# A two-block transformer on one core: the modulation's sums over partitions by 32x32 turns on VectorE and stacked identities, its gates by way of DRAM

## The chip, the core and the metric

The kernel runs on one core of one Trainium2 chip. The metric is the device time of one execution in microseconds (us); a kernel's time is the median of its runs. TensorE (PE) multiplies, VectorE (DVE) and ScalarE (ACT) do the elementwise work, GpSimd (POOL) a few small things, and SyncE (SP) issues nearly all transfers. PEld stands for TensorE's weight loads.

## What is computed

Two transformer blocks over 256 tokens of width 1024, in float32. The second block has two layers. In each, a vector `c` (one for the whole batch) is turned into six vectors of 1024, by which the layer's activations are shifted, scaled and gated. This modulation is what the change is about:

```python
c_act = jax.nn.silu(c)
for i in range(DEPTH_2):                                   # two layers
    mod = (c_act @ ada_w[i] + ada_b[i])[:, None, :]        # 1024 x 6144
    sh_a, sc_a, g_a, sh_f, sc_f, g_f = jnp.split(mod, 6, axis=-1)
    h = rms_norm(x, norm_g[i, 0]) * (1.0 + sc_a) + sh_a
    y = ...                                                # one of two attentions of h
    x = x + g_a * rms_norm(y, norm_g[i, 1])
    h = rms_norm(x, norm_g[i, 2]) * (1.0 + sc_f) + sh_f
    x = x + g_f * rms_norm(swiglu_2(h, ffn_w_in[i], ffn_w_out[i]), norm_g[i, 3])
```

## The kernel before

**The products.** All weights (42 million numbers, and 13 million of the modulation) are read once. SP loads them in tiles `raw` (three buffers, each of four units of 128x512); ACT rounds each unit to a high part `hi`, DVE subtracts to a low part `lo`, and TensorE forms each product from matmuls of high by high, high by low and low by high parts, mostly of 512 columns, through `mm` (line 145 in the profile). Turns of activations are `transpose` calls through `tr` (line 151). `hi` and `lo` have 16 pairs of buffers (`slots`), and further ones (`wp`) in the feed-forward parts.

**What sets the order.** The class `Order` writes the program in one pass. It keeps a clock `o.now` that runs with TensorE's matmuls, and small generators (tasks) are resumed when the clock has reached the time that they gave. `pin` ties each instruction to the one before it on its engine, so the order in which tasks happen to issue is each engine's order on the chip. All work of DVE, ACT and POOL is recorded at line 89, all transfers at line 137. The planned durations only set the order; on the chip every instruction still waits for its own inputs. A transfer carries one of eight completion semaphores in turn, so a transfer also waits until the one eight before it has landed.

**The modulation (`ada`).** The product `c_act @ ada_w` isn't made on TensorE. For each of 12 vectors, in two halves of 512, four transfers bring 128x2x512 weights to `araw`, and DVE adds them into `sums` (tiles `asum`) with 8 `scalar_tensor_tensor` operations by `c_act`. Each of the 128 partitions then holds a part of the sum, and `ada_finish` adds over the partitions, once for each of the 24 halves:

- for the 16 halves of shifts and scales: four 128x128 turns of `sums` on TensorE into a bank, one `reduce_sum` on DVE from the bank to four columns of `fm`, and for the scales one small operation with the norm's gain;
- for the 8 halves of gates: `split` of `sums` to a high and a low part (one ACT copy, one DVE subtraction), two matmuls of 512 columns with an all-ones matrix `ones_r`, which leave the sum in every partition, and one DVE product into a tile `gain` that holds the norm's gain, read by `load_gain` as one row sent to all partitions.

`chain` uses `gain` after a projection or feed-forward part, and `evacuate` uses `fm`.

**The start.** SP issues the halves of `x`, the first four weight units, then seven small transfers of vectors (`rows`, 8 or 12 rows of 128 numbers each, later turned into columns by `turn_rows`), and then the next weight tile.

**An address pad.** `small("pad_end", [P, PAD_END])` takes 104 numbers per partition, so that the tiles allocated behind it (`qp`, `gp`, `wp`) begin at a chosen address.

Of the kernel before, what the change touches and what calls it, by code (L numbers as in the profile page):

```python
# [12 lines left out]
F32 = mybir.dt.float32  # L13
F32R = mybir.dt.float32r
AF = mybir.ActivationFunctionType
OP = mybir.AluOpType
AX = mybir.AxisListType
# [3 lines left out]
P = 128  # L21
D = 1024
# [11 lines left out]
STOCK = 9  # L34
ADA_START, ADA_EARLY, ADA_LATE = 30.0, 5.5, 8.0
HEADS_1, HEADS_2 = 9.0, 2.0
PAD_END = 104
FIRST_DMA, SLOW_BYTES = 1.9, 2.2e6
RATE, SLOW_RATE = 360e3, 270e3
WARM = 6  # L40
# [178 lines left out]
def block_kernel(ctx: ExitStack, tc: tile.TileContext, a: dict, onehot: bass.AP, out: bass.AP):  # L219
    nc = tc.nc  # L220
    o = Order(tc)
    A, V, G = o.A, o.V, o.G
# [4 lines left out]
    dram = ctx.enter_context(tc.tile_pool(name="dram", bufs=1, space=DRAM))  # L227

    def ring(pool, name, n, shape, dtype=F32):
        return Ring([pool.tile(shape, dtype, name=f"{name}{i}") for i in range(n)])  # L230

    def small(name, shape, dtype=F32):
        return cst.tile(shape, dtype, name=name)

    banks = ring(psum, "bank", 8, [P, 512])
    raws = ring(cst, "raw", 3, [P, 2048])
    araws = ring(cst, "araw", 2, [P, 1024])
    slots = Ring([(small(f"hi{i}", [P, 512], F32R), small(f"lo{i}", [P, 512], F32R)) for i in range(16)])
    st = ring(cst, "st", 4, [P, 528])
    ch = ring(cst, "ch", 3, [P, 512])  # L240
    ep = ring(cst, "ep", 4, [P, 384])
    gains = ring(cst, "gain", 2, [P, D])
    asum = ring(cst, "asum", 2, [P, 512])
# [119 lines left out]
    def split(hi, lo, src, after=0.0):  # L363
        t = A.activation(hi, src, AF.Copy, after=after)
        return V.tensor_sub(lo, src, hi.bitcast(F32), after=t)
# [75 lines left out]
    vec = {}  # L441
# [29 lines left out]
    def stay_warm():  # L471

        b = banks.take()
        for _ in range(WARM):
# [8 lines left out]
    later = rows(("c", a["c_2"].rearrange("l (k p) -> (l k) p", p=P), 8),  # L483
                 ("conv", a["conv_w"].rearrange("l t (k p) -> (l t k) p", p=P), 12),
                 ("ffn_pre", a["norm_ffn_pre"].rearrange("l (k p) -> (l k) p", p=P), 8),
                 *((("g", l, i), a["norm_g_2"][l, i].rearrange("(k p) -> k p", p=P), 8) for l in range(2) for i in (0, 2)))
    ident = small("ident", [P, P])
    make_identity(nc, ident)
    tri = small("tri", [P, P])
    nc.vector.memset(tri, 1.0)  # L490
    ones_r = small("ones_r", [P, P], F32R)
# [114 lines left out]
    def load_gain(src, gain):  # L606
        gain.tile = yield from o.get(gains)
        gain.load.t = o.dma(gain.tile, src.to_broadcast([P, D]))


    fm = [small(f"fm{l}", [P, 4, 8]) for l in range(2)]
# [3 lines left out]
    ada_done = {one: [Mark(), Mark()] for one in ada_order}  # L615
    gated = {one: Gain() for one in ada_order if one[1][0] == "g"}
# [2 lines left out]
    c_mark = Mark()  # L619
    c_act = small("c_act", [P, 8])  # L620

    def ada_finish(l, what, cc, sums, r):
        yield r
        c = slice(cc * 512, (cc + 1) * 512)
        if what[0] == "g":
            yield from o.until(gated[l, what].load)
            pair = yield from o.get(slots)
            hv, lv = pair
            r = split(hv, lv, sums)
            asum.give(sums, r)  # L630
            yield r
            tp = yield from o.get(banks)
            o.mm(tp, ones_r, hv, True, False)
            r = o.mm(tp, ones_r, lv, False, True)
            slots.give(pair, r)
            yield r
            dst = gated[l, what].tile[:, c]
            r = V.tensor_mul(dst, dst, tp)
        else:
            tp = yield from o.get(banks)  # L640
            for j in range(4):
                r = o.tr(tp[:, j * P:(j + 1) * P], sums[:, j * P:(j + 1) * P], ident)
            asum.give(sums, r)
            yield r
            i = {"sh_a": 0, "sc_a": 1, "sh_f": 2, "sc_f": 3}[what]
            dst = fm[l][:, i, cc * 4:cc * 4 + 4]
            r = V.reduce_sum(dst, tp.rearrange("p (k c) -> p k c", c=P), axis=AX.X)
            if what[1] == "c":
                yield r
                g = vec["g", l, 0 if what == "sc_a" else 2][:, cc * 4:cc * 4 + 4]  # L650
                r = V.scalar_tensor_tensor(dst, dst, 1.0, g, op0=OP.add, op1=OP.mult)
        banks.give(tp, r)
        ada_done[l, what][cc].t = r

    def ada():
        yield from o.until(c_mark)
        pieces = [(l, what, cc, k0) for l, what in ada_order for cc in range(2) for k0 in range(0, 8, 2)]
        loaded, t0 = [], o.now
        for i in range(len(pieces) + 1):
            if i < len(pieces):  # L660
                l, what, cc, k0 = pieces[i]
                c0 = parts_of.index(what) * D + cc * 512
                if k0 == 0:
                    if what[0] == "g" and cc == 0:
                        o.spawn(load_gain(a["norm_g_2"][l, 1 if what == "g_a" else 3].unsqueeze(0), gated[l, what]))
                    sums = yield from o.get(asum)
                    r = G.memset(sums, 0.0)
                    yield r
                    ba = o.dma(sums[0:1, :], a["ada_b_2"][l:l + 1, c0:c0 + 512])
                t = yield from o.get(araws)  # L670
                arrival = o.dma(t.rearrange("p (k c) -> p k c", c=512),
                                a["ada_w_2"][l].rearrange("(k p) c -> p k c", p=P)[:, k0:k0 + 2, c0:c0 + 512])
                loaded.append((l, what, cc, k0, t, max(arrival, ba), sums))
            if i:
                l, what, cc, k0, t, arrival, s = loaded.pop(0)
                yield max(arrival, t0 + i * ADA_EARLY)
                while (o.urgent or V.free > o.now + SLACK or
                       pos["lo"] - pos["first"] < STOCK and o.now < t0 + i * ADA_LATE):
                    yield o.now + 0.2
                for k in range(2):  # L680
                    r = V.scalar_tensor_tensor(s, t[:, k * 512:(k + 1) * 512], c_act[:, k0 + k:k0 + k + 1], s,
                                               op0=OP.mult, op1=OP.add)
                    yield r - 0.3
                araws.give(t, r)
                if k0 == 6:
                    o.spawn(ada_finish(l, what, cc, s, r), r)


    def scope(**kinds):

        stack, got = ExitStack(), {}
        for name, (n, shape, dtype) in kinds.items():
            got[name] = ring(stack.enter_context(tc.tile_pool(name=name, bufs=1, reuse_waits="tile")), name, n, shape, dtype)
        return stack, got
# [87 lines left out]
    cum, cum_mark = [small(f"cum{h}", [P, 8]) for h in range(2)], [Mark(), Mark()]  # L782
    rows_mark = Mark()

    small("pad_end", [P, PAD_END])
    phase, sc = scope(qp=(4, [P, 4, 256], F32), gp=(8, [P, 512], F32),
                                   mk=(1, [P, 256], F32))
    qks, gp = sc["qp"], sc["gp"]
# [209 lines left out]
    group(take(2), 260, keep_gb, None)  # L998
    o.spawn(gates_of_c())
    o.spawn(ada(), ADA_START)  # L1000
    group(take(2), 512, keep_gc, None)
    group(take(2), 512, make_z, None)
# [428 lines left out]
```

## Time and profile before

| what | us |
|---|---|
| median of 3 runs | 981.91 (981.43 to 982.16) |
| the profiled execution | 983.57 |
| its span, first to last instruction | 981.8 |
| TensorE busy in the span | 970.9 (99%) |
| VectorE busy | 773.7 (79%) |
| ScalarE busy | 622.3 (63%) |

TensorE runs at its full clock throughout (granted clock 0.999). A matmul's row in the profile gives its whole passage through the array, which overlaps the next one's; what it costs the stream is the distance from its start to the next start. Rows of a timeline merge equal instructions that follow each other; an instruction of float32 operands that isn't a turn stands there as two records.

### The profile page before, as it was taken

The numbers are of one execution on the slowest core, as the hardware profiler recorded it, in microseconds if no ns is written. First come the engines' busy times: TensorE is split into PE (matmuls) and PEld (weight loads), VectorE is DVE, ScalarE is ACT, GpSimd is POOL, SyncE is SP. The second block draws the span as 40 slices with busy tenths as digits, with TensorE's granted clock in tenths as the row PEclk, the third lists the DMA queues.
The fourth block names the chain that finished last, engine by engine and source line by source line (L and its number), as shares of the span: only waits on it lengthen the run. The fifth ranks groups of instructions, "written<-read, shape, count | busy, mean of one in ns | idle before, by whom it ended". The sixth has DMA issues, their size and how long they took to land.

```text
span 981.8 us, 14543 instructions
## 1 busy us (share of the span) xinstructions
PE 970.9 (99%) x4986; PEld 810.4 (83%) x4986; DVE 773.7 (79%) x1582; ACT 622.3 (63%) x1390; POOL 34.7 (4%) x65
## 2 busy tenths in 40 slices
PE   8999999999999999999999999999999999999997
PEld 6888778888888888888888888888887888888886
DVE  6689888889999977787899999867686797575742
ACT  6746676775555547866785555557888786565631
POOL 1000000000000001000000000001000100000000
PEclk9999999999999999999999999999999999999999
DMA  7977777669988975766769998874542667646401
GB/s 228 331 258 255 265 273 248 218 229 327 334 294 294 311 263 176 268 223 200 250 205 313 315 318 278 286 258 162 196 142 81 196 198 260 204 162 211 158 28 44
DMA packets 143639, 227.24 MB, mean 231 GB/s; under 512 B 6087, under 2 KB 79028, under 8 KB 143564
## 3 DMA queue, kind: packets, MB, share of 16 engines
q1 hardware_dynamic: 143548, 226.30, 68.6%
q8 instruction: 39, 0.64, 0.3%
q14 instruction: 36, 0.29, 0.1%
q10 hardware_dynamic: 16, 0.00, 0.0%
HBM read 225.22 MB, written 2.63 MB: 232 GB/s over the span
## 4 chain that ended last, share of the span: by engine, by line
PE 93%; issue 2%; DMA 2%; ACT 1%; DVE 1%; SPq 0%; POOL 0%; DVEq 0%; POOLq 0%; ACTq 0%
PE bank L145 89%; PE bank L151 4%; ACT hi L89 1%; DMA bf<-in_b_f_dram 1%; DMA x<-in_x_dram 1%; DVE lo L89 0%; SPq L137 0%; ACT junk L89 0%; DMA raw<-in_w_in_dram 0%; DVE x L89 0%; DVE ch L89 0%; POOL tiny L89 0%; ACT L89 0%; ACT hTb L89 0%; DVE hTb L89 0%
## 5 line engine op out<-in xcount | busy, mean ns | idle before, releaser
L89 DVE TENSOR_TENSOR lo<-raw,hi 128x512 fp32r<-128x512 f32 (+1 forms) x493 | 320.2, 676 | 25.6 <-ACT hi L89 21.2
L89 ACT ACTIVATE hi<-raw 128x512 fp32r<-128x512 f32 (+1 forms) x493 | 287.8, 618 | 43.6 <-PE bank L145 13.9
L145 PE MATMUL bank<-hi,hTb 128*128 128x512 f32 (+1 forms) x820 | 259.5, 389 | 0.9 <-ACT hTb L89 0.9
L145 PE MATMUL bank<-hTb,hi 128*128 128x512 f32 x612 | 219.7, 398 | 0.0
L145 PE MATMUL bank<-hi,pair 128*128 128x512 f32 x540 | 177.1, 392 | 0.0
L145 PEld LDWEIGHTS bank<-hi,hTb 128*128 128x128 f32 x820 | 150.4, 188 | 30.2 <-issue 1.5
L145 PE MATMUL bank<-hTb,lo 128*128 128x256 f32 x612 | 172.9, 283 | 0.0
L145 PE MATMUL bank<-lo,hTb 128*128 128x512 f32 (+1 forms) x410 | 159.3, 389 | 0.0
L89 DVE SCALAR_TENSOR_TENSOR asum<-araw,c_act,asum 128x512 f32<-128x512 f32 x192 | 143.0, 745 | 6.1 <-DMA araw<-in_ada_w_dram 5.5
L145 PEld LDWEIGHTS bank<-hTb,hi 128*128 128x128 f32 x612 | 114.9, 188 | 27.0 <-issue 0.3
L145 PEld LDWEIGHTS bank<-hi,pair 128*128 128x128 f32 x540 | 101.0, 188 | 21.2 <-issue 0.2
L145 PEld LDWEIGHTS bank<-hTb,lo 128*128 128x128 f32 x612 | 115.6, 189 | 1.7 <-issue 0.7
L89 ACT ACTIVATE wp<-raw 128x512 fp32r<-128x512 f32 x151 | 91.3, 626 | 28.0 <-PE bank L145 18.1
L145 PE MATMUL bank<-hTb,wp 128*128 128x512 f32 (+1 forms) x568 | 108.6, 339 | 0.0
L145 PE MATMUL bank<-lo,pair 128*128 128x512 f32 x270 | 105.9, 392 | 0.0
L89 DVE TENSOR_TENSOR wp<-raw,wp 128x512 fp32r<-128x512 f32 x151 | 99.4, 685 | 4.0 <-ACT wp L89 3.3
L89 ACT ACTIVATE st<-bank 128x256 f32<-128x256 f32 (+1 forms) x104 | 37.8, 397 | 100.8 <-PE bank L145 100.7
L145 PEld LDWEIGHTS bank<-hTb,wp 128*128 128x128 f32 x568 | 87.3, 188 | 13.1
L145 PEld LDWEIGHTS bank<-lo,hTb 128*128 128x128 f32 x410 | 77.1, 188 | 14.0 <-issue 0.5
L145 PE MATMUL bank<-wp,pair 128*128 128x512 f32 x270 | 70.0, 393 | 0.0
L89 DVE TENSOR_TENSOR st<-st,bank 128x256 f32<-128x256 f32 x96 | 39.0, 414 | 37.2 <-ACT st L89 37.2
L145 PEld LDWEIGHTS bank<-lo,pair 128*128 128x128 f32 x270 | 50.7, 188 | 9.9
(133 smaller groups left out, 884.6 us busy)
## 6 DMA issues: line engine op xcount, KB each, us to landing
araw<-in_ada_w_dram SPq DMA_DIRECT2D x96, 512.0 KB
raw<-in_ffn_w_in_dram SPq DMA_DIRECT2D x88, 512.0 KB
raw<-in_w_gate_up_dram SPq DMA_DIRECT2D x44, 512.0 KB
raw<-in_ffn_w_out_dram SPq DMA_DIRECT2D x22, 1024.0 KB
raw<-in_w_in_dram SPq DMA_DIRECT2D x16, 1024.0 KB
raw<-in_moba_w_qkv_dram SPq DMA_DIRECT2D x12, 1024.0 KB
raw<-in_diff_w_qkv_dram SPq DMA_DIRECT2D x12, 1024.0 KB
raw<-in_w_down_dram SPq DMA_DIRECT2D x11, 1024.0 KB
```

The costliest lines, as they stand in the source:

```text
L89: self.order.pin(self, fn(out, *args, **kw))
L145: self.pin(self.pe, self.nc.tensor.matmul(out, lhsT, rhs, start=start, stop=stop, skip_group_check=shared))
L151: self.pin(self.pe, self.nc.tensor.transpose(out, src, ident))
```

## The change

The sums over partitions are made otherwise, and for a whole vector at a time:

- Each half: DVE turns `sums` in blocks of 32x32 (`V.transpose`) into a tile `st`, and adds over the last index of each block into 16 columns of a tile `fold`. Now the sum over 128 partitions is a sum over four blocks of 32.
- Each vector, when both halves are there: four small float32 matmuls with `stacked` (four 32x32 identities one below the other, 128x32) add the four blocks and put each quarter of the vector at its partitions, 128x8 in all.
- For shifts and scales one DVE operation moves this to `fm`. For gates DVE multiplies it with the norm's gain (now also a column vector, so `rows` reads four more vectors at the start) into `gate`; SP writes `gate` to DRAM (`gate_d`), and 14 planned us later reads it back as one row sent to all partitions (`gain`). `load_gain` is no longer used for the gates.
- `pad_end` goes; the new small tiles take as much room (32 + 32 + 32 + 8 = 104 numbers). `qp`, `gp`, `wp`, `hi`, `lo`, `hTb` and `pair` keep their addresses; `ident` and other small tiles move by 128 to 416 bytes.

```diff
-PAD_END = 104
...
-                 *((("g", l, i), ..., 8) for l in range(2) for i in (0, 2)))
+                 *((("g", l, i), ..., 8) for l in range(2) for i in range(4)))
     ident = small("ident", [P, P])
     make_identity(nc, ident)
+    stacked = small("stacked", [P, 32])
+    for q in range(4):
+        nc.vector.tensor_copy(stacked[q * 32:(q + 1) * 32], ident[q * 32:(q + 1) * 32, q * 32:(q + 1) * 32])
...
+    folded = Ring([(small(f"fold{i}", [P, 32]), Mark(), Mark()) for i in range(1)])
+    fold_of, gate = {}, small("gate", [P, 8])
+    gate_d = dram.tile([4, D], F32, name="gate_d")
+
     def ada_finish(l, what, cc, sums, r):
         yield r
-        c = slice(cc * 512, (cc + 1) * 512)
+        if not cc:
+            fold_of[l, what] = yield from o.get(folded)
+            for m in fold_of[l, what][1:]:
+                m.t = None
+        while (l, what) not in fold_of:
+            yield o.now + 0.1
+        one = fold_of[l, what]
+        z = yield from o.get(st)
+        r = V.transpose(z[:, :512], sums)
+        asum.give(sums, r)
+        yield r
+        r = V.reduce_sum(one[0][:, cc * 16:(cc + 1) * 16], z[:, :512].rearrange("p (b j) -> p b j", j=32), axis=AX.X)
+        st.give(z, r)
+        one[1 + cc].t = r
+        if not cc:
+            return
+        yield from o.until(*one[1:])
+        tp = yield from o.get(banks)
+        for q in range(4):
+            r = o.mm(tp[q * 32:(q + 1) * 32, :8], stacked, one[0].rearrange("p (k q) -> p q k", q=4)[:, q], True, True)
+        folded.give(one, r)
+        yield r
         if what[0] == "g":
-            yield from o.until(gated[l, what].load)
-            pair = yield from o.get(slots)
-            hv, lv = pair
-            r = split(hv, lv, sums)
-            asum.give(sums, r)
-            yield r
-            tp = yield from o.get(banks)
-            o.mm(tp, ones_r, hv, True, False)
-            r = o.mm(tp, ones_r, lv, False, True)
-            slots.give(pair, r)
-            yield r
-            dst = gated[l, what].tile[:, c]
-            r = V.tensor_mul(dst, dst, tp)
+            i = (0 if what == "g_a" else 1) + 2 * l
+            r = V.tensor_mul(gate, tp[:, :8], vec["g", l, 1 if what == "g_a" else 3])
+            banks.give(tp, r)
+            yield r + 3.0
+            yield o.dma(gate_d[i:i + 1].rearrange("o (k p) -> p (o k)", p=P), gate) + 14.0
+            gain = gated[l, what]
+            gain.tile = yield from o.get(gains)
+            r = o.dma(gain.tile, gate_d[i:i + 1].to_broadcast([P, D]))
         else:
-            tp = yield from o.get(banks)
-            for j in range(4):
-                r = o.tr(tp[:, j * P:(j + 1) * P], sums[:, j * P:(j + 1) * P], ident)
-            asum.give(sums, r)
-            yield r
             i = {"sh_a": 0, "sc_a": 1, "sh_f": 2, "sc_f": 3}[what]
-            dst = fm[l][:, i, cc * 4:cc * 4 + 4]
-            r = V.reduce_sum(dst, tp.rearrange("p (k c) -> p k c", c=P), axis=AX.X)
             if what[1] == "c":
-                yield r
-                g = vec["g", l, 0 if what == "sc_a" else 2][:, cc * 4:cc * 4 + 4]
-                r = V.scalar_tensor_tensor(dst, dst, 1.0, g, op0=OP.add, op1=OP.mult)
-        banks.give(tp, r)
-        ada_done[l, what][cc].t = r
+                r = V.scalar_tensor_tensor(fm[l][:, i], tp[:, :8], 1.0, vec["g", l, 0 if what == "sc_a" else 2],
+                                           op0=OP.add, op1=OP.mult)
+            else:
+                r = V.tensor_copy(fm[l][:, i], tp[:, :8])
+            banks.give(tp, r)
+        for m in ada_done[l, what]:
+            m.t = r
...
-                    if what[0] == "g" and cc == 0:
-                        o.spawn(load_gain(a["norm_g_2"][l, 1 if what == "g_a" else 3].unsqueeze(0), gated[l, what]))
...
-    small("pad_end", [P, PAD_END])
```

What this does to the order, at three places. First SP near the start of the program, before: the last small vectors (tile `ep`), the second weight tile (`raw_72`, in four units), and what each waits for (`DMAHW0` to `DMAHW7` are the eight completion semaphores).

```order
L137 DMA ep_116<-in_norm_ffn_pre_dram 8x128 [waits DMAHW3_49]
L137 DMA ep_116<-in_norm_g_dram 8x128 [waits DMAHW4_49]
L137 DMA ep_116<-in_norm_g_dram 8x128 [waits DMAHW5_49]
L137 DMA ep_116<-in_norm_g_dram 8x128 [waits DMAHW6_49]
L137 DMA ep_116<-in_norm_g_dram 8x128 [waits DMAHW7_49]
L137 DMA raw_72<-in_w_in_dram 128x512 [waits DMAHW0_49]
L137 DMA raw_72<-in_w_in_dram 128x512 [waits DMAHW1_49]
```

The same place of SP after the change:

```order
L136 DMA ep_116<-in_norm_ffn_pre_dram 8x128 [waits DMAHW3_49]
L136 DMA ep_116<-in_norm_g_dram 8x128 [waits DMAHW4_49]
L136 DMA ep_116<-in_norm_g_dram 8x128 [waits DMAHW5_49]
L136 DMA ep_116<-in_norm_g_dram 8x128 [waits DMAHW6_49]
L136 DMA ep_116<-in_norm_g_dram 8x128 [waits DMAHW7_49]
L136 DMA ep_116<-in_norm_g_dram 8x128 [waits DMAHW0_49]
L136 DMA ep_116<-in_norm_g_dram 8x128 [waits DMAHW1_49]
L136 DMA ep_116<-in_norm_g_dram 8x128 [waits DMAHW2_49]
L136 DMA ep_116<-in_norm_g_dram 8x128 [waits DMAHW3_49]
L136 DMA raw_72<-in_w_in_dram 128x512 [waits DMAHW4_49]
L136 DMA raw_72<-in_w_in_dram 128x512 [waits DMAHW5_49]
```

Four small transfers more stand ahead of `raw_72`; its first unit now waits for the transfer that stood eight before it in the new count. ACT's and TensorE's order up to there is the same in both.

Second, TensorE before, in the projection of the first block where the second vector of layer 0 is added (the four turns of `asum_122` are one half of it):

```order
L145 MATMUL bank_64<-qp_224,qp_226 128x128
L145 MATMUL bank_64<-qp_224,qp_226 128x256
L145 MATMUL bank_66<-hi_78,hTb 128x512
L151 MATMUL bank_68<-ident,asum_122 128x128 x4
L145 MATMUL bank_66<-lo_79,hTb 128x512
L145 MATMUL bank_66<-hi_78,hTb 128x512
```

TensorE after, where the same vector is added now:

```order
L144 MATMUL bank_64<-lo_97,pair_164 128x512
L144 MATMUL bank_64<-hi_96,pair_165 128x512
L144 MATMUL bank_64<-hi_98,pair_164 128x512
L144 MATMUL bank_69<-fold_220,stacked 32x8 x4
L144 MATMUL bank_64<-lo_99,pair_164 128x512
L144 MATMUL bank_64<-hi_98,pair_165 128x512
```

The vector's two groups of four turns have become one group of four small matmuls, and it stands later, among the products of `w_branch`; the ten matmuls in front of it (three are shown) fill `bank_64`, and the product in `bank_66` ends just before those ten.

Third, DVE before, around the reduction that belongs to these turns:

```order
L89 TENSOR_TENSOR pair_167<-bank_63,pair_166 128x256
L89 ISA ep_115,tiny_144<-bank_64,mk_242 128x128
L89 ISA tiny_144 128x1
L89 ISA ep_115,tiny_144<-bank_64,mk_242 128x256
L89 TENSOR_REDUCE fm_208<-bank_68 128x4
L89 TENSOR_TENSOR lo_77<-raw_71,hi_76 128x512
```

DVE after, around the turn and the reduction that the group above waits for:

```order
L88 SCALAR_TENSOR_TENSOR asum_122<-araw_75,c_act,asum_122 128x512 x2
L88 TENSOR_TENSOR pair_167<-bank_70,pair_166 128x256
L88 STREAM_TRANSPOSE st_110<-asum_122 128x512
L88 TENSOR_TENSOR gp_244<-gp_244,bank_66 128x512
L88 TENSOR_REDUCE fold_220<-st_110 128x16
L88 TENSOR_TENSOR lo_85<-raw_72,hi_84 128x512
```

DVE's reduction moved from behind TensorE's turns to ahead of TensorE's group, with a turn of its own before it and one product that waits for TensorE (`bank_66`) between the two.

## Rows read from the trace of the kernel before

**Rows 1.** The page's first part: busy us (share of span) xinstructions.

```profile
PE 970.9 (99%) x4986; PEld 810.4 (83%) x4986; DVE 773.7 (79%) x1582; ACT 622.3 (63%) x1390; POOL 34.7 (4%) x65
```

**Rows 2.** TensorE's waits: who for whom; us in total, times, longest.

```profile
PE bank L145 <- DVE logf L89: 1.1, 1, 1.1
PE bank L145 <- ACT hTb L89: 0.9, 1, 0.9
PE bank L151 <- DVE ch L89: 0.4, 1, 0.4
```

**Rows 3.** Groups by form: count | busy us, mean ns | idle before.

```profile
L151 PE MATMUL bank<-ident,asum 128*128 128x128 f32 x64 | 9.6, 272 | 0.0
...
L145 PE MATMUL bank<-hi,ones_r 128*128 128x512 f32 x8 | 3.3, 416 | 0.0
```

**Rows 4.** TensorE's timeline at 162 us: start, us, line, names, xcount.

```profile
162.02 0.39 PE L145 MATMUL bank<-lo,pair 128*128 128x512 f32 x1
162.25 0.60 PE L151 MATMUL bank<-ident,asum 128*128 128x128 f32 x4
162.60 0.71 PE L145 MATMUL bank<-hi,pair 128*128 128x512 f32 x2
163.15 0.40 PE L145 MATMUL bank<-lo,pair 128*128 128x512 f32 x1
```

**Rows 5.** TensorE's timeline at 693 us, a gate's half.

```profile
693.52 0.40 PE L145 MATMUL bank<-hi,ones_r 128*128 128x512 f32 x1
693.75 0.40 PE L145 MATMUL bank<-lo,ones_r 128*128 128x512 f32 x1
693.98 0.39 PE L145 MATMUL bank<-hi,hTb 128*128 128x512 f32 x1
```

**Rows 6.** TensorE's timeline at 112 us, around weights of 33x8.

```profile
112.24 0.39 PE L145 MATMUL bank<-lo,hTb 128*128 128x512 f32 x1
112.56 0.81 PE L145 MATMUL bank<-st,tab 33*8 33x384 f32 x2
113.30 0.73 PE L145 MATMUL bank<-hi,hTb 128*128 128x512 f32 x2
113.87 0.40 PE L145 MATMUL bank<-lo,hTb 128*128 128x512 f32 x1
```

**Rows 7.** TensorE's timeline at 41 us: float32 by 8 columns.

```profile
41.07 0.37 PE L145 MATMUL bank<-logf,tri 128*128 128x8 f32 x2
41.30 0.71 PE L145 MATMUL bank<-hi,hTb 128*128 128x512 f32 x2
```

**Rows 8.** TensorE's timeline, weights of 64 columns: one head, then two together.

```profile
107.06 0.86 PE L145 MATMUL bank<-ep,gp 128*64 128x256 f32 x4
...
127.27 0.88 PE L145 MATMUL bank<-ep,gp 128*64 128x256 f32 x8
```

**Rows 9.** SP's timeline at the start: issues of transfers.

```profile
4.99 0.31 SPq L137 DMA_DIRECT2D ep<-in_conv_w_dram  x1
5.35 0.28 SPq L137 DMA_DIRECT2D ep<-in_norm_ffn_pre_dram  x1
7.22 3.32 SPq L137 DMA_DIRECT2D ep<-in_norm_g_dram  x4
10.91 1.78 SPq L137 DMA_DIRECT2D raw<-in_w_in_dram  x4
```

**Rows 10.** ACT's timeline at 14 us; in brackets idle time and what ended it.

```profile
13.69 0.63 ACT L89 ACTIVATE hi<-raw 128x512 fp32r<-128x512 f32 x1 [1.26 <-DMA raw<-in_w_in_dram]
...
14.84 0.40 ACT L89 ACTIVATE hTb<-ch 128x256 fp32r<-128x256 f32 x1
```

**Rows 11.** TensorE's timeline at 15 us.

```profile
15.29 0.50 PE L145 MATMUL bank<-hi,hTb 128*128 128x512 f32 x1 [0.89 <-ACT hTb L89]
```

**Rows 12.** Groups by form on DVE.

```profile
L89 DVE TENSOR_REDUCE fm<-bank 128x4 f32<-128x512 f32 x16 | 11.0, 688 | 4.0 <-PE bank L151 4.0
...
L89 DVE TENSOR_TENSOR lo<-asum,hi 128x512 fp32r<-128x512 f32 x8 | 5.5, 691 | 4.9 <-ACT hi L89 4.8
```

**Rows 13.** SP's waits, the longest in total.

```profile
SPq L137 <- DVE lo L89: 328.6, 100, 20.2
```

**Rows 14.** SP's timeline at 119.8 us: a transfer of 1024 rows.

```profile
119.80 1.33 SPq L137 DMA_DIRECT2D rep_d<-line_d  x1
```

More of the change, by code (lines that the diff above doesn't have):

```diff
@@ L485, in block_kernel @@
                  ("ffn_pre", a["norm_ffn_pre"].rearrange("l (k p) -> (l k) p", p=P), 8),
-                 *((("g", l, i), a["norm_g_2"][l, i].rearrange("(k p) -> k p", p=P), 8) for l in range(2) for i in (0, 2)))
+                 *((("g", l, i), a["norm_g_2"][l, i].rearrange("(k p) -> k p", p=P), 8) for l in range(2) for i in range(4)))
     ident = small("ident", [P, P])
     make_identity(nc, ident)
+    stacked = small("stacked", [P, 32])
+    for q in range(4):
+        nc.vector.tensor_copy(stacked[q * 32:(q + 1) * 32], ident[q * 32:(q + 1) * 32, q * 32:(q + 1) * 32])
     tri = small("tri", [P, P])
```

## The prediction

> **What bounds the kernel now.** I read the page's busy times first, then TensorE's waits, then starts in its timeline. TensorE is busy 970.9 us of 981.8 [rows 1]. Of its few waits the reader should note which come after the first 20 us: 1.1 us for `logf` at 40 us and 0.4 us for `ch` [rows 2]; the 0.9 us for `hTb` belong to the start [rows 11]. DVE (773.7 us) and ACT (622.3 us) [rows 1] hardly ever keep TensorE waiting. So the time is TensorE's stream, and an edit is worth what it takes from or adds to that stream, plus what it does to the first 20 us, where transfers set the pace. What an instruction costs the stream is the distance of starts: a 512-column matmul 162.25 - 162.02 = 0.23 us, though its own row says 0.39 [rows 4].
>
> **What is removed from TensorE.** Four turns take 162.60 - 162.25 = 0.35 us, and the two matmuls behind them 163.15 - 162.60 = 0.55 instead of 2 x 0.23 = 0.46, so a group costs 0.44 [rows 4]. There are 64 turns of `asum` [rows 3], 16 groups: 16 x 0.44 = 7.0 us. A gate's half is 693.98 - 693.52 = 0.46 us [rows 5]; eight halves (eight `hi` by `ones_r`, and as many `lo`) [rows 3]: 8 x 0.46 = 3.7 us. No idle time stood before either [rows 3], so all of it was stream: -10.7 us.
>
> **What is added to TensorE.** Twelve groups of four float32 matmuls with weights of 128x32 and 8 columns: eight records a group. The trace has no such shape, so I price it from two neighbours.
>
> The first is the fixed part of using a small piece of the array between full-width matmuls. With weights of 33x8 [rows 6], the matmul ahead takes 112.56 - 112.24 = 0.32 instead of 0.23 (+0.09); the two records take 113.30 - 112.56 = 0.74, where 2 x 384 columns at the turns' 0.44 / 512 = 0.86 ns a column would be 0.66 (+0.08); the two matmuls behind take 113.87 - 113.30 = 0.57 instead of 0.46 (+0.11). That is 0.28 us around the group, whatever is in it. The Trainium skill, TensorEngine Tiling (Array Packing), section Key Properties, has a rule that speaks against this change: changing the tiling mode drains TensorE. By that rule, the trace agrees: 0.28 us. Without it the twelve groups would be 12 x 0.28 = 3.4 us cheaper, and the sum would come to 974.6.
>
> The second is the eight records. Two records of 8 columns with full weights (128 columns) take 41.30 - 41.07 = 0.23 us, 0.115 each [rows 7]; eight at that price are 0.92 us, the upper end. For the lower end: one head's four records with weights of 64 columns span 0.86 us, and eight records of two heads, on the two halves of the array, 0.88 [rows 8]. A second column piece adds 0.02 while the first works. The four matmuls of a group write to four different quarters of partitions, so they should overlap too: two records of one, 2 x 0.115 / 4 = 0.06 if the price is that of the weights' columns (32 instead of 128), and three pieces more at 0.02: 0.12 us. Eight one after the other at a quarter of 0.115 would be 0.23. I take 0.17, between these two, because the heads' rows are the nearest. A group is 0.28 + 0.17 = 0.45 us (0.40 to 1.20), twelve are **+5.4 us** (4.8 to 14.4).
>
> **The start.** SP issues small transfers 5.35 - 4.99 = 0.36 us apart [rows 9]. Four more stand ahead of `raw_72`, which was issued at 10.91 [rows 9], right after the last of them: 4 x 0.36 = 1.4 us later, so at 12.3. The completions that the first units then wait for are those of small transfers issued from 7.22 on [rows 9]; I take them as landed by then. ACT waited 1.26 us for `raw_72` until 13.69, and only behind that copy in its order comes the copy into `hTb` at 14.84 [rows 10], for which TensorE waited 0.89 us until 15.29 [rows 11]. ACT's order is unchanged there, so the delay goes through: **+1.4 us**. It can be nothing, if the landing isn't what the copy really waits for, and 2.2 if the first units also wait for a completion. What follows (`logf` at 40 us) hangs on products of TensorE made after the delay, so I don't expect its 1.1 us of waiting to give anything back.
>
> **What is hidden.** DVE loses 16 reductions of 688 ns, eight low halves of 691 [rows 12] and eight products as long, about 22 us; it gains 24 turns and 24 reductions of 512 columns, at 0.69 us each 33 us. The 11 us more lie beside TensorE, spread over two thirds of the kernel, and DVE's results are seldom what TensorE waits for [rows 2]. If the cover were gone they would cost up to 11 us; what speaks for it is that DVE stood busy 79% [rows 1] and TensorE didn't wait. ACT loses eight copies. The gates' writes have 1024 pieces of four bytes each. The longest comparable issue on SP, of 1024 rows, took 1.33 us [rows 14]; four such are 5 us of a queue that waits 328.6 us for DVE alone [rows 13]. The wait of the reading transfer for the write can hold up the weight loads queued behind it on SP, but 14 planned us lie between, and the rows of the order show weight loads there: nothing. The turn of 92 instead of 60 rows and the four copies of `stacked` at the start, which DVE makes before its first real work, I take as nothing; one group of turns is 0.44. `ident` moves by 128 bytes; no row shows what an address does to a turn, and I let up to 1.0 us stand to either side (a few per cent of the few hundred turns of 0.11 us that remain).
>
> **Sum.** -7.0 - 3.7 + 5.4 + 1.4 = -3.9 us. Against the profiled execution, 983.57 (1.8 around its span of 981.8), that is 979.7; against the median, 981.91, it is **978.0 us**.
>
> **Rivals.**
>
> - *The records of a group don't overlap.* Four matmuls share the moving tile and one bank, and the heads that overlapped had banks and operands of their own in part. At half of 0.115 us for each of eight records, 0.46 + 0.28 = 0.74 a group, 8.9 us in all: -10.7 + 8.9 + 1.4 = -0.4, **981.5 us**, no change. For it: with full weights records do come 0.115 apart [rows 7]. Against it: the second head's 0.02 [rows 8]. The Trainium skill, TensorE: Matmul & The Clock Gate, section Wait — 56ns, not 53.3ns?, knows such a floor: about 62 ns of the sequencer for each matmul where it decodes in microcode; by that figure the estimate is 8 x 0.062 + 0.28 = 0.78 a group and 982.0 us. The second head's records in rows 8 speak against it. Chance 0.10.
> - *Slower: the full price for each record.* If weights of 32 columns load no faster than of 128 and nothing overlaps, a group is 0.92 + 0.28 = 1.20 us, twelve are 14.4, and the sum is +5.1: **987.0 us**. The kernel becomes slower than measurable from (10.7 - 1.4 + 2.0) / 12 = 0.94 us a group on. For it speaks only that the trace has no weights of 32 columns with few columns to move. Chance 0.06.
> - *TensorE waits for DVE at the groups.* Before, it made the turns itself, right behind DVE's additions; now two DVE operations more stand between. At the tightest place, that shown in the change's order, ten matmuls (2.3 us) lie between the product in `bank_66` and the group, and DVE must do a product and a reduction behind it, 1.4 us and the hand-overs. If the 32x32 turn is much longer than 0.69 us, or the reduction with 16 outputs, waits of 0.3 us at each of twelve groups give +3.6 back: **981.6 us**. Chance 0.10.
> - *The start hides the small transfers.* If another input of `hTb` is what ends last there, or the later wait for `logf` shrinks by as much, the 1.4 us vanish: **976.6 us**. Chance 0.09.
>
> **How the numbers follow.** About 0.2% (2 us) is what a measurement of this kernel can tell from no change. The forecast has 0.65. Range: the low end is the start hidden and groups at 0.40 less the turns' 1.0 (975.0), which I don't let in whole: 975.6. The high end takes in the first and third rival, 981.7; left out are the slower rival and some of the tails. Faster: nearly all of the forecast, the last rival and a small part of the third, 0.74. Within: the first and most of the third, and a forecast that comes out too small, 0.19. Slower: 0.07.
>
> **What would show it.** In the changed kernel's timeline: the start of the matmul behind each group of `fold` by `stacked`, to the one ahead of it, should show 0.45 us more than matmuls alone, the rows of the group starting close together; twelve groups, no idle time named before them. `raw_72`'s issue should stand at 12.3 and TensorE's wait for `hTb` grow from 0.9 to 2.3. TensorE's waits should else stay as they are. The prediction fails if new waits for weights appear around the gates' writes (SP held up by `gate_d`), if a group costs near 0.9 us, or if the distance of starts of the plain 512-column matmuls isn't 0.23 any more.

## The result and the profile after

The changed kernel takes **1000.62 us** (median; 998.15 to 1003.0) against 981.93 of the kernel before measured beside it: the ratio is 1.0185, with a 95% interval of 1.0172 to 1.0198. The forecast was 978.0 with a range up to 981.7. The forecast missed the direction, and the time by 22.6 us. Its profiled execution took 999.62 us with a span of 997.9; before it was 983.57 and 981.8.

The page of the changed kernel: TensorE's busy time, the transfers, and the chain that ended last by engine, against [rows 1] of before.

```profile
PE 972.7 (97%) x5002; PEld 806.4 (81%) x5002; DVE 784.0 (79%) x1606; ACT 617.6 (62%) x1382; POOL 35.4 (4%) x65
...
DMA packets 147862, 227.27 MB, mean 228 GB/s; under 512 B 10279, under 2 KB 83252, under 8 KB 147788
...
PE 84%; DMA 7%; DVE 3%; ACT 3%; issue 2%; SPq 0%; POOL 0%; DVEq 0%; POOLq 0%; ACTq 0%
```

TensorE is busy 972.7 us, hardly more than the 970.9 of before, but in a span 16 us longer. The chain, which before was TensorE for 93% and transfers for 2%, is now transfers for 7%. There are some 4200 packets more under 512 bytes (6087 before): the four gate writes with their 1024 pieces each.

TensorE's waits in the changed kernel (who for whom; us in total, times, longest), against [rows 2]:

```profile
PE bank L150 <- DVE ep L88: 7.1, 2, 4.4
PE bank L150 <- DVE st L88: 3.2, 1, 3.2
PE bank L144 <- DVE fold L88: 2.9, 1, 2.9
PE bank L144 <- ACT hTb L88: 2.0, 1, 2.0
```

Before, nothing past the first 45 us waited longer than 0.4 us. Now there are four waits of 2.7 to 4.4 us, at 364, 578, 680 and 789 us. The four `gate_d` writes were issued at 321.9, 541.7, 660.2 and 768.9 us, so each wait comes 20 to 42 us behind one. And TensorE is not back at once: these are stretches of the trace before and behind the first two waits (us from and to, length, busy time and count of PE, PEld, DVE, ACT, POOL, then the granted clock, DMA share and GB/s).

```profile
359.00:364.00 5.00, 0.78 (x4) 0.32 (x2) 5.00 (x11) 4.03 (x10) 0.00 (x0) 0.99 0.81 280
364.00:369.00 5.00, 4.82 (x16) 3.94 (x17) 4.75 (x9) 1.87 (x4) 0.00 (x0) 0.67 0.86 265
...
574.00:579.00 5.00, 2.13 (x19) 1.66 (x18) 5.00 (x10) 1.42 (x4) 0.53 (x1) 0.99 1.07 382
579.00:584.00 5.00, 5.00 (x21) 4.25 (x20) 4.12 (x9) 3.12 (x7) 0.00 (x0) 0.67 0.92 315
```

Behind the four waits the granted clock of the next 4 to 5 us is 0.57 to 0.67 in the mean: a part of it at 1.2 GHz, the rest at 2.4. Behind each of these two that costs 5 x 0.33 = 1.7 us on top of the wait. Note also DVE: while TensorE waits "for DVE" here, DVE is busy all 5.00 us. It isn't slow; it works off a pile that came late.

What was late shows in the throughput around the first write (a digit of DMA share and the GB/s for each half microsecond from 318 on; the write is issued at 321.87, in the eighth of them):

```profile
DMA  9999964239589969606197974946356987999999
GB/s 358 344 365 371 342 231 168 82 41 82 147 344 325 135 17 10 4 0 33 35 74 57 49 33 47 53 27 12 35 39 94 111 152 234 354 397 389 393 399 383
DMA packets 3662, 3.38 MB, mean 169 GB/s; under 512 B 1139, under 2 KB 2905, under 8 KB 3660
```

From 325 to 333 us the transfers move some 35 GB/s instead of 350, although loads are queued: SP issued weights at 324.17 and 327.88. SP's own issues get stuck there too (start, duration):

```profile
321.87 0.85 SPq L136 DMA_DIRECT2D gate_d<-gate  x1
...
329.77 4.22 SPq L136 DMA_DIRECT2D asum<-in_ada_b_dram  x1
334.09 1.59 SPq L136 DMA_DIRECT2D araw<-in_ada_w_dram  x1
```

The write's own issue took only 0.85 us. About 8 us at a tenth of the rate are some 2.5 MB that come late. The stock of converted weights hides it first; then ACT and DVE, which work in a fixed order, stand behind missing `raw` and `araw` loads, and TensorE, also in a fixed order, waits for whatever small product of DVE is next: `ep`, `st` or `fold`. The name in the list of waits is only the last link. In the chain that ended last each of the four waits stands behind a load (start, length):

```profile
348.29 7.85 DMA raw<-in_w_down_dram
...
547.45 13.20 DMA araw<-in_ada_w_dram
...
662.33 13.59 DMA raw<-in_diff_w_qkv_dram
...
774.05 13.02 DMA raw<-in_ffn_w_in_dram
```

### The profile page after: what moved, and what is told of

Its sections match the earlier page's. It is cut to its first block, busy times and chain, and to the rows that moved or that the text cites. A ratio compares the mean times of both kernels' runs of the same rounds, so it can differ in the third digit from the quotient of the medians.

```text
span 997.9 us, 14525 instructions
## 1 busy us (share of the span) xinstructions
PE 972.7 (97%) x5002; PEld 806.4 (81%) x5002; DVE 784.0 (79%) x1606; ACT 617.6 (62%) x1382; POOL 35.4 (4%) x65
## 4 chain that ended last, share of the span: by engine, by line
PE 84%; DMA 7%; DVE 3%; ACT 3%; issue 2%; SPq 0%; POOL 0%; DVEq 0%; POOLq 0%; ACTq 0%
PE bank L144 81%; PE bank L150 3%; DMA raw<-in_ffn_w_in_dram 2%; DMA raw<-in_diff_w_qkv_dram 1%; DMA araw<-in_ada_w_dram 1%; ACT hi L88 1%; DVE lo L88 1%; DMA raw<-in_w_down_dram 1%; DMA bf<-in_b_f_dram 1%; DVE asum L88 1%; DMA x<-in_x_dram 1%; DVE st L88 0%; SPq L136 0%; ACT junk L88 0%; DVE wp L88 0%
## 5 line engine op out<-in xcount | busy, mean ns | idle before, releaser
L88 DVE TENSOR_TENSOR lo<-raw,hi 128x512 fp32r<-128x512 f32 (+1 forms) x481 | 312.2, 676 | 29.4 <-ACT hi L88 26.5
L88 ACT ACTIVATE hi<-raw 128x512 fp32r<-128x512 f32 (+1 forms) x481 | 280.1, 617 | 70.7 <-PE bank L144 20.6
L144 PE MATMUL bank<-hTb,hi 128*128 128x512 f32 x596 | 215.1, 399 | 0.0
L144 PE MATMUL bank<-hi,pair 128*128 128x512 f32 x516 | 172.1, 397 | 0.0
L88 ACT ACTIVATE wp<-raw 128x512 fp32r<-128x512 f32 x163 | 97.1, 625 | 46.2 <-DMA raw<-in_w_down_dram 16.3
L144 PE MATMUL bank<-hTb,wp 128*128 128x512 f32 x600 | 114.7, 339 | 0.0
L88 DVE TENSOR_TENSOR wp<-raw,wp 128x512 fp32r<-128x512 f32 x163 | 106.4, 685 | 9.6 <-ACT wp L88 8.3
L144 PEld LDWEIGHTS bank<-hTb,wp 128*128 128x128 f32 x600 | 92.6, 188 | 14.3
L144 PE MATMUL bank<-wp,pair 128*128 128x512 f32 x306 | 79.1, 396 | 0.0
L144 PEld LDWEIGHTS bank<-wp,pair 128*128 128x128 f32 x306 | 57.1, 191 | 12.3
```

Of the source, the lines that this page charges most:

```text
L88: self.order.pin(self, fn(out, *args, **kw))
L144: self.pin(self.pe, self.nc.tensor.matmul(out, lhsT, rhs, start=start, stop=stop, skip_group_check=shared))
```

## The experiments

Theory T: the 1024 pieces of 4 bytes of each gate write take the throughput away, and everything else follows. Rivals: R1, the longer way of the sums through DVE; R2, the transfer that reads the gates back and waits for the write on SP; R3, small pieces as such; R4, the changed order of TensorE's work.

**Undo the pieces, leave all else.** The two sides of one pattern change places, so that the gates come back permuted; the instruction order of TensorE is the same, and so is every address.

```
-yield o.dma(gate_d[i:i + 1].rearrange("o (k p) -> p (o k)", p=P), gate) + 14.0
+yield o.dma(gate_d[i:i + 1].rearrange("o (p k) -> p (o k)", p=P), gate) + 14.0
```

> The changed kernel with one number different: each gate's 4 KB are written as 128 pieces of 32 bytes (every partition's eight values together) instead of 1024 of 4 bytes. Every engine keeps its order and every tile its place; what is left out is the right order of the gate's values in DRAM, so the gates that come back are permuted. Theory T (the number of pieces is what holds the transfers up): a write lands in 3 to 5 us, none of the four waits of 2.7 to 4.4 us is left, and the time is the sum without them, 982 - 10.8 + 4.5 + 1.3 = 977.0; 975.5 to 980. Rival R3 (pieces under some size are slow however few): 990 to 1001. Rival R4 (the changed order of TensorE's work is what makes it wait): 995 to 1001.

Measured: 977.65 us, ratio 0.9963 (0.9948 to 0.9977). All four waits are gone, and the clock is 0.999. The longest waits that are left, of which the first two belong to the first 16 us:

```profile
PE bank L144 <- ACT hTb L88: 1.8, 1, 1.8
PE bank L474 <- DVE junk L468: 1.3, 1, 1.3
PE bank L144 <- DVE logf L88: 0.3, 1, 0.3
```

The throughput from 317 on, with the write at 320.31:

```profile
GB/s 330 334 348 389 361 168 45 53 168 246 381 222 57 0 78 274 338 274 375 385 375 326 313 221 172 188 190 305 354 387 389 406 385 285 233 254 438 397 418 401
DMA packets 4065, 5.63 MB, mean 282 GB/s; under 512 B 294, under 2 KB 2812, under 8 KB 4063
```

So R1, R2, R3 and R4 are out as causes: DVE's way, the read, the order and 32-byte pieces are all still there.

**Add only the pieces, to the kernel before.** A spawned step writes 4 KB that nobody reads, 3 us behind each finished gate.

```
+    def unused(l, what):
+        i = (0 if what == "g_a" else 1) + 2 * l
+        o.dma(gate_d[i:i + 1].rearrange("o (k p) -> p (o k)", p=P), vec["g", l, 0])
...
+            if cc:
+                o.spawn(unused(l, what), r + 3.0)
```

> The kernel before, with four writes of 1024 pieces of 4 bytes added, each 3 us behind a finished gate, of a tile that is there anyway into DRAM that nobody reads. Theory T: each takes about 11.5 us to land, the loads behind it come late, and the time rises by what the changed kernel lost against its sum, 1000.6 - 977 = 23.6 with the lower clock; 996 to 1008. Rival R1 (DVE's way): 982 to 984, since nothing else is changed and an issue on SP costs at most 1.33 us of a queue that waits. Rival R2 (the read that waits for the write): 982 to 986, since nothing reads the writes.

Measured: 1001.34 us, ratio 1.019 (1.017 to 1.021). That is 19.0 us more than the 982.35 beside it, as much as the changed kernel lost in all (18.7 us), without any other part of the change. (In the changed kernel the same writes cost more, 22.5 us; the section on the prediction has the sum.) Its waits:

```profile
PE bank L151 <- issue: 5.9, 1, 5.9
PE bank L151 <- ACT ch L89: 4.1, 1, 4.1
PE bank L145 <- DVE st L89: 1.8, 1, 1.8
PE bank L151 <- DVE ep L89: 1.6, 1, 1.6
```

Other names than in the changed kernel, the same cause. The throughput from 294 to 314 us, of the kernel before and then of this one (write at 297.59):

```profile
GB/s 410 361 176 29 0 0 33 106 115 299 367 307 363 375 299 346 385 381 375 336 303 358 371 387 389 385 389 385 344 135 188 377 369 401 426 148 209 242 283 371
```

```profile
DMA  0004779899999999999499668999668883999999
GB/s 8 0 0 61 102 250 291 264 361 381 379 330 358 293 166 278 223 63 16 10 35 51 39 53 55 59 64 51 63 115 127 123 115 90 283 307 350 397 389 410
```

The digits tell more than the GB/s: from 302.5 to 310.5 us the DMA engines are mostly 60% busy or more while they move 65 GB/s. They are not idle, and yet it is not the pieces that keep them busy. Packets and busy share of the engines in this kernel, first from 297.5 to 302.5 us, then from 302.5 to 310.5 (the share adds up the packets' times, so it can pass 100%):

```profile
DMA packets 2473, 1.52 MB, mean 303 GB/s; under 512 B 1088, under 2 KB 2381, under 8 KB 2473
q1 hardware_dynamic: 2473, 1.52, 121.8%
...
DMA packets 524, 0.52 MB, mean 65 GB/s; under 512 B 16, under 2 KB 524, under 8 KB 524
q1 hardware_dynamic: 524, 0.52, 98.0%
```

The pieces go through first, at 303 GB/s in all; in the trace each takes 9 ns. Behind them it is the packets of loads that take long: 98% of 16 engines for 8 us are 125 us, for 524 packets 0.24 us each, where a load's packet of 1024 bytes mostly takes 0.05 us. Where the written pieces stand meanwhile, the trace does not show.

**Another queue.** `gate) + 14.0` becomes `gate, A) + 14.0`: ACT issues the write.

> The changed kernel, with the four gate writes issued by ACT instead of SP, so that they stand in another queue; still 1024 pieces of 4 bytes. Theory T in the form Tq (only what stands behind the pieces in the same queue is late): loads keep their usual 3.5 to 5 us, the waits behind the writes go, 977 to 982. In the form Td (the 16 DMA engines or the memory behind them are what is slow, whoever issued): throughput falls as before during some 10 us, the waits stay, 995 to 1003.

Measured: 997.01 us, 1.0149 (1.0129 to 1.0168); from 325 to 333 us (the fifteenth value on) the transfers move between 2 and 80 GB/s:

```profile
GB/s 369 379 350 289 385 391 320 74 16 74 184 344 341 92 6 14 2 2 4 23 55 80 66 37 35 45 31 10 33 27 76 68 111 186 234 375 385 406 401 397
```

The form Td holds: what is slow is shared. The Trainium skill, DMA: Bandwidth & Descriptors, section Issuing engines are not separate DMA queues, says that transfers run on the same 16 engines whoever issues them; the trace agrees.

**What is it about the pieces?** Five variants of the unread writes in the kernel before, each with the order of TensorE unchanged. First half as many pieces, `[:, :4]` of either side:

> The kernel before with four unread writes of 512 pieces of 4 bytes, half of those that made it 1001.3. Theory T with a price for each piece: throughput falls for about 5 instead of 10 us behind each; what waits lose falls by more than half, since the stock of converted weights covers some microseconds: 983 to 991. If a write of such pieces has a fixed price: 997 to 1003.

Measured: 994.77 us, 1.0128 (1.0109 to 1.0148): +12.6 us by the ratio, against +18.7 by the ratio for all of them. Half the pieces cost two thirds; this fell between both expectations. Next, 1024 pieces loaded from DRAM instead of written to it:

```
+        o.dma(unread, a["norm_g_2"][l, 1].rearrange("(k p) -> p k", p=P))
```

> The kernel before with four loads of 1024 pieces of 4 bytes (a row of norm weights of 4 KB into a tile that nobody uses) where the unread writes were. If it is the count of pieces that holds up the transfers, in either direction: 995 to 1005. If it is the writing of pieces into DRAM: 982 to 985.

Measured: 981.92 us, 0.9999 (0.9989 to 1.0008). Loading by pieces of 4 bytes costs nothing here. Next, the writes with their pieces apart, in a tile of `[4, D, P]` and one of `[4, D, 16]`, of which only `[i, :, 0]` is written:

> The kernel before with the four unread writes of 1024 pieces of 4 bytes (which made it 1001.3), the pieces now 512 bytes apart in DRAM instead of one behind the other. Theory Tn (each piece has its price, wherever it lands): as with neighbours, 997 to 1005. Theory Ts (neighbours in the same stretch of DRAM wait for each other): the writes pass in 1 to 3 us and the time is 982 to 986.

> The kernel before with the four unread writes of 1024 pieces of 4 bytes, the pieces 64 bytes apart in DRAM: with pieces one behind the other it came to 1001.3, with pieces 512 bytes apart to 981.5. If what counts is that pieces share 64 bytes: 981 to 985. If it is a wider stretch, 512 bytes for example: 990 to 1003.

Measured: 981.54 us, 1.0 (0.999 to 1.0009), with 512 bytes between them; 982.14 us, 0.9998 (0.9989 to 1.0008), with 64 bytes. The same count of pieces of the same size, and no loss. At last neighbours that come from one partition (the source takes every second value of a tile, so that the pieces stay apart):

> The kernel before with four unread writes of 1024 pieces of 4 bytes which lie one behind the other as in the writes that made it 1001.3, but the eight values of a partition, every second one of a tile, stand side by side, instead of 128 partitions' values. If any neighbours hold each other up: 992 to 1003. If only neighbours that come from different partitions, and so in parts at the same time, do: 982 to 986.

Measured: 1003.89 us, 1.0219 (1.0174 to 1.0264). The throughput from 294 on of 512 bytes apart, of 64 bytes apart, and of one partition's values side by side:

```profile
GB/s 401 385 365 209 25 8 0 49 106 225 328 270 326 367 356 307 360 329 199 222 377 340 289 383 356 375 393 395 393 406 324 320 393 393 426 377 82 74 98 246
```

```profile
GB/s 53 33 57 143 176 319 277 358 377 352 307 367 313 168 209 328 236 338 379 346 373 381 401 389 389 352 287 410 410 401 426 189 98 90 295 295 369 379 381 391
```

```profile
GB/s 86 45 12 0 135 160 258 295 283 389 377 377 356 338 164 181 260 139 20 31 14 18 43 76 74 53 143 154 82 72 47 33 61 102 127 301 369 367 381 410
```

What costs is hundreds of 4-byte pieces written side by side in DRAM. At 64 bytes from piece to piece they cost nothing measurable, and whether neighbours come from one partition or from many makes no difference that these runs can tell. Not shown is what makes neighbours slow: pieces that share one stretch of 64 bytes, or very many pieces within a few KB. No run lies between 4 and 64 bytes, and 1024 larger pieces side by side were not tried.

**The rest of the change.** The four loads more at the start, alone in the kernel before (`for i in range(4)`, late pools kept in place):

> The kernel before with the four rows of norm weights more loaded at the start, as the changed kernel does (92 rows instead of 60 are turned at once); nothing else, late pools in their place. The prediction's term for the start was 1.4 us: 983.3; by the traces of the kernels with the four loads TensorE waits 1.3 to 2.0 us for hTb, against 0 to 0.9 without: 982.7 to 984. If the start hides them: 982.0.

Measured: 983.8 us, 1.0018 (1.0008 to 1.0028): +1.8 us. Next, a contiguous write by way of a turn on TensorE:

```
+            r = o.tr(tp[:8, :P], gate, ident)
+            r = V.tensor_copy(e[:8, :P], tp[:8, :P])
+            r = o.dma(gate_d[i:i + 1].rearrange("o (k p) -> (o k) p", p=P), e[:8, :P])
```

> The changed kernel, with one thing different: each gate is turned on TensorE (128x8 to 8x128, four turns in all) and written to DRAM as 8 rows of 512 bytes instead of 1024 pieces of 4 bytes. Theory T (the pieces hold up the transfers that are issued with and behind them, the loads come about 10 us late, ACT and DVE after them, and TensorE waits and runs at a lower clock for a while): the writes land in about 2 to 4 us, the four waits of 2.7 to 4.4 us behind them go, and the time is 982 - 10.8 + 4.5 (12 groups of 0.38) + 1.3 (start) + 1.5 (four turns with their copies) = 978.5, 977 to 981. Rival R1 (the way of the sums through DVE, with two operations more, makes TensorE wait): 998 to 1002, since DVE has even one operation more. Rival R2 (not the write but the transfer that reads it back holds SP up): 990 to 1002, since the read still waits for the write.

Measured: 984.61 us, 1.0027 (1.0017 to 1.0036), 3.6 us over the range that T gave. The waits behind the writes are gone, and at 735 to 742 us the same matmuls start 4.8 to 5.8 us earlier than in the kernel before. Then the planner, whose state the new steps have moved, places the work of the second attention differently. TensorE's timeline:

```profile
762.97 2.84 PE L144 MATMUL bank<-gp,ptp 128*128 128x128 f32 x24
765.57 0.47 PE L144 MATMUL bank<-hi,pair 128*128 128x512 f32 x1
767.70 0.66 PE L150 MATMUL bank<-ident,st 128*128 128x128 f32 x4 [1.66 <-DVE st L88]
770.46 0.50 PE L144 MATMUL bank<-hi,pair 128*128 128x512 f32 x1 [2.10 <-ACT pair L88]
```

24 value matmuls stand in a row, and then one matmul, while ACT, POOL and DVE work some 2 us at the norm that the turn of `st` needs. No load stands in the chain that ended last there, so these waits are the planner's, not the write's; this run confounds two things, and the one with 128 pieces, in which the order stays, is the cleaner test.

The turns' half of the change without any gate in DRAM, once with late pools 128 bytes lower, once in their place (`small("pad_end", [P, 32])`):

> Half of the change alone: shifts and scales go through DVE's turns and the fold as in the changed kernel, the gates through ones_r and the two matmuls a half as in the kernel before; no gate goes through DRAM, and the four rows of norm weights more are not loaded. Theory T: 982 - 7.0 (64 turns) + 8 x 0.38 = 978.0, 976.5 to 980. Rival R1 (the way through DVE makes TensorE wait): two thirds of the groups remain, 990 to 996.

> The kernel with the gates as before and the turns of shifts and scales through DVE, which came to 981.1 where the sum was 978.0, with 128 bytes a partition of unused space ahead of the late pools, so that these stand where they stand in the kernel before. Theory P (the places of TensorE's tiles set the pitch of its matmuls; it was 229 ns in the middle there, against 227 of before): 977 to 979.5. If the places don't matter: 980.5 to 982, and the missing 3 us are elsewhere.

Measured: 981.14 us, 0.9984 (0.9975 to 0.9993), and 979.34, 0.9977 (0.9967 to 0.9986). By the ratios that is 1.6 and 2.3 us better than before, where 4 were expected. The intervals overlap, so the places were tried by themselves: the kernel before with `PAD_END = 72`.

> The kernel before with 128 bytes a partition less of unused space ahead of the late pools, as in the kernel with the gates as before that came to 981.1, and nothing else: every engine's order is the same. Theory P (the places of tiles set the pitch of TensorE's matmuls): plain matmuls of 512 columns go from 227 to 229 ns in the middle, 1.0 to 3.5 us more: 983 to 985.5. If the places don't matter: 981.5 to 982.4.

Measured: 983.2 us, 1.0016 (1.0006 to 1.0026): +1.6 us with every instruction in its order, so places do count. The two traces show where. 24 matmuls with weights from `wp`, one of the late pools, and the row behind them, first in the kernel before, then in this one:

```profile
789.72 5.60 PE L145 MATMUL bank<-wp,hTb 128*128 128x512 f32 x24
795.16 0.39 PE L145 MATMUL bank<-hi,hTb 128*128 128x512 f32 x1
...
789.26 5.75 PE L145 MATMUL bank<-wp,hTb 128*128 128x512 f32 x24
794.85 0.39 PE L145 MATMUL bank<-hi,hTb 128*128 128x512 f32 x1
```

The starts lie (795.16 - 789.72) / 24 = 0.227 us apart before and (794.85 - 789.26) / 24 = 0.233 here. Over all 480 matmuls with weights from `wp` the traces differ by 2.0 us; the median distance behind matmuls with weights from `hi` and `lo`, which did not move, is 0.227 in both. Why the place of the weights does this is not shown. The kernel with the gates as before still misses some 1.5 us of its sum with its pools in place; that stays open.

**A version that beats both.** One matmul gives a gate as 32 rows of 32 values, and its norm weights come late:

```
+        if what[0] == "g":
+            r = o.mm(tp[:32, :32], one[0], stacked, True, True)
...
+            o.dma(gate, a["norm_g_2"][l, 1 if what == "g_a" else 3].rearrange("(b i) -> b i", i=32))
...
+            yield o.dma(gate_d[i:i + 1].rearrange("o (b i) -> (o b) i", i=32), gate) + 14.0
```

> A version meant to be faster than both: as the changed kernel, but a gate's four matmuls of 128x32 by 8 columns become one, with the fold as weights and the stacked identities as moving tile; it gives the gate as 32 rows of 32 values, which go to DRAM as 32 pieces of 128 bytes. Its norm weights are loaded in the same form shortly before, so that the four loads at the start go; tiles of TensorE keep the places of before. Theory T: 982 - 10.8 + 8 x 0.38 + 4 x 0.45 = 976.0, 974.5 to 978.5. Rival R1 (DVE's way makes TensorE wait): 985 or more.

Measured: **977.29 us**, ratio 0.996 (0.9945 to 0.9975), 4.7 us less than the 981.95 beside it.

## Why the prediction was wrong, step by step

**The step that failed** is the sentence on the gates' writes in "What is hidden". It took the issue of a transfer of 1024 rows, 1.33 us [rows 14], as the price of four writes of 1024 pieces, found it covered by SP's waiting [rows 13], and put down nothing. The issue was not priced too low (it took 0.46 to 0.85 us each). But the issue is only what SP spends; the price of this transfer was what it took from all other transfers, and no row of before shows such a write. The term got no bounds from either side, so the range had nothing to hold the result. The 14 planned us between write and read cover the write's landing for the one who reads; they do nothing for the weights behind it. The prediction did name the sign of it ("new waits for weights appear around the gates' writes"), with the wrong mechanism: not SP held up by a wait, but throughput.

The size of that term, from the spans of the changed kernel and the one with 128 pieces: 997.9 - 975.4 = 22.5 us. TensorE's idle time past 300 us is 14.3 us in the one and 0.1 in the other. The clock behind four waits lost 1.7 + 1.7 + 1.7 + 1.7 = 6.7 us (5 x 0.33, 5 x 0.33, 5 x 0.34, 4 x 0.43). Their sum is 20.9; 1.0 more is waiting at the start, which varies from execution to execution, and 0.6 stays open.

The Trainium skill, DMA: Bandwidth & Descriptors, section Specifications, states that under 512 bytes a transfer is below line rate because of a read-modify-write. It bears on this and wasn't weighed. It speaks of every small transfer, and of its own rate, not of what the others lose; the runs are narrower: 32-byte pieces and 4-byte pieces 64 bytes apart cost nothing measurable (977.65 and 982.14), four writes of 1024 neighbours of 4 bytes 19 us. No run here shows whether a read-modify-write is behind it.

**What held.** *Removed turns and halves less groups.* The group, in the changed kernel's timeline:

```profile
101.45 0.61 PE L144 MATMUL bank<-hi,hTb 128*128 128x512 f32 x2
101.99 0.25 PE L144 MATMUL bank<-fold,stacked 128*32 128x8 f32 x8
102.17 0.50 PE L144 MATMUL bank<-lo,hTb 128*128 128x512 f32 x1
102.51 0.63 PE L144 MATMUL bank<-hi,hTb 128*128 128x512 f32 x2
```

From 101.45 to 102.51 are 1.06 us with three plain matmuls, 0.69: the group costs 0.37 instead of 0.45, twelve 4.4 instead of 5.4. Its eight records take 0.18, near the value chosen between both ends (0.17); around them it is 0.19 (0.08 ahead, 0.11 behind) instead of the 0.28 read from the rows of 33x8. The rivals of records one behind the other, at 0.46 and 0.92, fall.

*The start.* `raw_72` was issued behind eight small transfers, against [rows 9]:

```profile
7.67 4.06 SPq L136 DMA_DIRECT2D ep<-in_norm_g_dram  x8
11.78 2.80 SPq L136 DMA_DIRECT2D raw<-in_w_in_dram  x6
```

At 11.8, not 12.3; TensorE's wait for `hTb` grew from 0.89 [rows 11] to 2.0, not 2.3. Timed alone it is 1.8 (0.8 to 2.7) against 1.4. The step held, and the rival in which the start hides it falls.

*DVE.* Its turns took 704 ns and its reductions 678, as the 0.69 that were taken, and in the kernel with 128 pieces TensorE never waits for them. The rival "TensorE waits for DVE at the groups" seemed to come true at 578 us (2.9 us for `fold`), but that wait vanishes with the pieces.

*Addresses.* `ident`'s turns still come 109 ns apart, as allowed for. That the late pools keep their place, which the change sees to, is worth 1.6 us (0.6 to 2.6); the 1.0 that was put on addresses was for `ident` alone.

With all this the kernel with 128 pieces, 977.65, lies 0.4 us from the forecast. That it is so near is in part luck: the groups came out 1.0 cheaper and the start 0.4 dearer, and the half of the change that was timed alone fell some 1.5 us short of its sum. What sank the forecast was a term put at nothing; measured, it is 22.5 us.

## What to carry to other kernels

Price a transfer twice: its issue on the queue, and what it takes from the transfers of everyone else; where the trace has no such transfer, let the range hold a bad value for it. A tile with one value a partition and column should not go to DRAM in 4-byte neighbours: turn it first, or choose a layout in which each partition writes 32 bytes in one piece, which cost nothing here. When TensorE waits for a small product of a busy engine, look some 20 to 40 us back in the GB/s line for what made that engine late.

## What the runs showed of the hardware

- Behind a write of 1024 pieces of 4 bytes side by side in DRAM all transfers together move some 25 to 70 GB/s for 7 to 10 us, on SP's queue or on ACT's. The DMA engines show as busy, with packets of loads that take 0.24 us each in the mean (from 302.5 to 310.5 us of the kernel with unread writes), not with the pieces. The same pieces 64 bytes apart, or loaded, or the same 4 KB as 128 pieces of 32 bytes, don't do this.
- The records of four float32 matmuls with 128x32 weights into four partition quarters of one bank start mostly 6 to 7 ns apart, and all eight records take 0.18 us.
- 128 bytes of shift of pools that TensorE reads changed the time by 1.6 us (0.6 to 2.6) with no instruction moved; in a row of 24 matmuls with shifted weights the starts lay 0.233 instead of 0.227 us apart.
- Behind a wait of 3 to 4 us TensorE's clock was 0.57 to 0.67 in the mean of the 4 to 5 us looked at (a part at 1.2 GHz); that adds 1.7 us, about half of the wait.
